# Key projections cut at column 256 instead of 272, and the gated activations' room moved by 192 bytes, in a hybrid attention block

## The chip, the cores and the metric

The kernel runs on one core of one Trainium2 chip. The metric is the device time of one execution in microseconds (us); lower is better. The time of a kernel is the median of its runs; the kernel before has three of them. A run of the profiler adds a trace: for every instruction of every engine its start, its duration and what it waited for. The engines are TensorE (PE, the matmuls; its weight loads are listed apart as PEld), VectorE (DVE), ScalarE (ACT), GpSimd (POOL) and the queue that issues the DMAs (SP).

## The reference

One decoder layer over 528 positions: 16 meta tokens ahead of 512 real ones, a model width of 1024. Cut to what matters here:

```
u = rmsnorm(h, pre_norm_g)
(cq, ckv, k_pe, z_mla, fq, fk, fv, f_logit, z_fox, gate_a, gate_b) = split(u @ w_in)
MLA: q from rmsnorm(cq) @ w_uq, k and v from rmsnorm(ckv) @ w_ukv, 16 heads, causal softmax
FoX: q, k, v = fq, fk, fv, 16 heads of 64, causal softmax with a forget gate in the logits
y_mla = (o_mla * silu(z_mla)) @ w_br_mla ;  y_fox = (o_fox * silu(z_fox)) @ w_br_fox
mixed = (sigmoid(gate_a) * y_mla + sigmoid(gate_b) * y_fox) @ w_out
out = h + rmsnorm(mixed, post_norm_g)          # the 16 meta rows are dropped
```

Everything is float32. The kernel reaches that precision by splitting each operand into a high part that TensorE takes as it is and a low part that is the rest, and by summing three products: high weights with high data, high weights with low data, low weights with high data. So every product of the reference is three matmuls in the trace, named by their operands (`fk<-uTh,wh`, `fk<-uTl,wh`, `fk<-uTh,wl`: out, then streamed operand, then stationary one).

## The kernel before

**Layout.** The normalised input lies transposed in two tiles, `uTh` and `uTl` (high and low part): 128 partitions, 8 blocks of the model dimension (`KD`), and in each block a row of 576 float32 columns, of which the first 48 are unused, the next 16 are the meta tokens and the last 512 the real positions. A row is 2304 bytes, nine times 256, and both tiles begin at a multiple of 256 bytes in the partition (17,152 and 35,584 in the program's allocation). So position 0 lies 192 bytes into a block of 256 bytes, and position 16, the first real one, at the beginning of a block; so does position 272, which is 1024 bytes further.

**Units.** `unit` emits one projection: for each slice of positions and each of the 8 blocks, three matmuls into one PSUM bank, and `done` when the slice is complete. Queries run over the 512 real positions at once. Keys and values run over all 528, which is more than a bank holds, so they are cut into two slices: `ALLT` gives positions 0 to 272 and 272 to 528. `hl_done` is the eviction of queries and keys: ScalarE copies the bank into the high half of the tile `hlk` (line 247), then VectorE subtracts that from the bank and writes the low half (line 249, in the trace under the helper's line 104). It runs once per slice.

**Attention.** The heads are taken in 8 pairs, and each pair has two stages: FoX (`br` 1), then MLA (`br` 0). TensorE's instructions are issued in the order in which the program names them; the other engines' order is made by a planner that heeds priorities. A stage begins with `scores`: three groups of PSUM banks, each filled for the two heads of the pair by turns. The first group holds the scores of query block 1 over key positions 0 to 272 and of block 3 over 0 to 240; the second block 0 over 0 to 144 and block 3 over 240 to 528; the third block 2 over 0 to 400:

```
((1, 0, 272, 0), (3, 0, CUT, 272))        # rooms acc
((0, 0, 144, 0), (3, CUT, L - CUT, 144))  # rooms b0, b1
((2, 0, 400, 0),)                         # rooms c0, c1
```

Each part is a query block, the first key position, a width and a place in the bank. A part is three sets of two matmuls (one per head): high queries with high keys, low queries with high keys, high queries with low keys. After the scores the stage fills TensorE with the projections of the next stages. In an MLA stage this filling is the next pair's FoX work, in this order: queries (8 steps), the first slice of the keys (8), the values (16), the second slice of the keys (8). So the second slice of the FoX keys is the last thing that TensorE does ahead of the scores that read them, in seven of the eight pairs; the first pair's keys are made in the opening part, with other work behind them. In a FoX stage the MLA keys are made earlier, with values and a gate projection behind them.

**Branch products.** After attention the two branches' outputs are multiplied by `w_br_mla` and `w_br_fox`. The gated activations of a branch are split into the tiles `gh` and `gl` (8 blocks of 512 columns each, 2048 bytes a row), from a pool `m2`, which is opened at byte 90,880, a multiple of 256. For the FoX branch `pair_py` computes two output blocks at a time from seven products of 256 columns by 512 rows of contraction: four of the seven stream `gh` and `gl` themselves (`A11`, `S1`, `A12`, `A22`), the other three stream sums that lie in `a1` and `a2`. There are four such pairs, so 4 x 4 x 12 = 192 matmuls of 256 columns stream `gh` or `gl`. The tiles `a1` and `a2` begin 192 bytes past a multiple of 256 (161,216 and 169,408 for their high parts). For the MLA branch `py` streams `gh` and `gl` in 192 matmuls of 512 columns. The split weights that stand in TensorE in all of these begin at multiples of 256 bytes.

The names and lines that the change touches: `KEYS` (new, beside `HALF`), `ALLT`, `hl_done` (lines 237 to 250), `k_fox` (line 255), `k_mla` (line 687), and the pool `m2` (line 1066).

Of the kernel before, what the change touches and what calls it, by code (L numbers as in the profile page):

```python
# [11 lines left out]
F32 = mybir.dt.float32  # L12
# [13 lines left out]
L = S + META  # L26
NH = 16
KD = D // 128
# [7 lines left out]
O_CQ, O_ZM, O_FQ, O_FK, O_FV, O_F, O_ZF, O_GA, O_GB = 0, 416, 1440, 2464, 3488, 4512, 4528, 5552, 6576  # L36
# [7 lines left out]
SF_STEP = 272  # L44
PN_STEP = 5
HALF = 272
CUT = 240
ROW = 64

# [6 lines left out]
def block_kernel(ctx: ExitStack, tc: tile.TileContext, x, meta_tokens, pre_norm_g, w_in, fox_forget_b,  # L56
# [32 lines left out]
    def dma(out, src, start=None):  # L89

        with tc.issue_after(sums_out[0]) if written[0] and sums_out else nullcontext():
            ins = (start or nc.sync.dma_start)(out=out, in_=src)
        if written[0]:
            tc.keep_in_program_order(ins)
        return ins.ins

    def mm(*a, **k):
        nc.tensor.matmul(*a, **k)  # L98
# [4 lines left out]
    def split_lo(eng, lo, src, hi):  # L103
        return eng.tensor_tensor(out=lo, in0=src, in1=f32(hi), op=ALU.subtract)  # L104
# [34 lines left out]
    def weights(srcs, wrap):  # L139

        st = {}

        def load():
            if "l" not in st:
                st["l"] = wload(srcs())

        def get():
            load()
            return wrap(wsplit(st["l"]))
        get.load = load  # L150
        return get

    def by_k(part, nk):

        h, l = (t.rearrange("p (k f) -> p k f", k=nk) for t in part)
        return (lambda k: h[:, k, :]), (lambda k: l[:, k, :])
# [20 lines left out]
    def unit(name, getw, act, nk, sls, done, banks=None):  # L177

        st = {}
        out = []  # L180

        def prep():
            if "w" not in st:
                st["w"] = getw()
            return True
        for i, sl in enumerate(sls):
            n = sl.stop - sl.start
            for k in range(nk):
                def fn(i=i, sl=sl, k=k, n=n):
                    if "b" not in st:  # L190
                        st["b"] = prep()
                        for load in getattr(out[0][1], "nxt", ()):
                            load()
                    if k == 0:
                        st["ps"] = (banks or acc)(f"{name}{i}")
                    ps = st["ps"][:, :n]
                    (wh, wl), (ah, al) = st["w"], act(k)
                    for q, (w, a) in enumerate(((wh, ah), (wh, al), (wl, ah))):
                        mm(ps, w(k), a[:, sl], start=(k == 0 and q == 0), stop=(k == nk - 1 and q == 2))
                    if k == nk - 1:  # L200
                        done(i, ps)
                out.append((3 * n / 2.4, fn))
        out[0][1].prep = prep
        if hasattr(getw, "load"):
            out[0][1].load = getw.load
        return out

    keybank = [None]
    REAL = [slice(META, L)]
    ALLT = [slice(0, HALF), slice(HALF, L)]  # L210

    def u_act(k):
        return uTh[:, k, :], uTl[:, k, :]
# [7 lines left out]
    def win_w(off, i):  # L221
        return weights(lambda: [win[:, :, off + 128 * i : off + 128 * i + 128]], lambda w: by_k(w[0], KD))
# [14 lines left out]
    def hl_done(key, n, w):  # L237

        def done(i, ps):
            if i == 0:  # L240
                hls[key] = hlp.tile([128, 2, n], F32R, tag=f"hl{key[0]}", name="hl" + "".join(map(str, key)))
            hl = hls[key]
            o = w * i
            w_ = min(w, n - o)

            with tc.high_priority(offset=30), tc.issue_after(normed[0]) if key == ("q", 0, 0) else nullcontext():
                halved[key, i] = nc.scalar.copy(hl[:, 0, o : o + w_], ps).ins
            with tc.high_priority(offset=30):
                lowered[key, i] = split_lo(nc.vector, hl[:, 1, o : o + w_], ps, hl[:, 0, o : o + w_]).ins
        return done  # L250
# [2 lines left out]
        return unit(f"fq{pr}", win_w(O_FQ, pr), u_act, KD, REAL, hl_done(("q", 1, pr), S, S))  # L253

    def k_fox(pr):
        return unit(f"fk{pr}", win_w(O_FK, pr), u_act, KD, ALLT, hl_done(("k", 1, pr), L, HALF), keybank[0])

# [1 line left out]
    with ExitStack() as ph:  # L261
# [246 lines left out]
        latent(2, sms[2])  # L508

        qk = q_fox(0) + k_fox(0)  # L510
        behind[:] = [squared[1]]
        run(qk[:7])
# [34 lines left out]
    with ExitStack() as att:  # L547
# [7 lines left out]
        def bank(tag):  # L555
            return lambda name: stp.tile([128, 512], F32, tag=tag, name=name)
# [4 lines left out]
        def two(tag):  # L561
            return lambda name: bank(tag + name[-1])(name)
# [121 lines left out]
        mw = {}  # L684

        def k_mla(pr):
            return unit(f"mk{pr}", lambda: by_k(mw[pr][2], 1), ckv_act, 1, ALLT, hl_done(("k", 0, pr), L, HALF), two("b"))

        vsc = {}

        def v_unit(br, pr):
# [39 lines left out]
            def tr():  # L731
                dma(vps[br], vh.rearrange("p t c -> p (t c)"), nc.sync.dma_start_transpose)
            return unit(f"v{br}{pr}", get, act, nk, ALLT, done, two("c")), [(0, tr)]

# [15 lines left out]
        def attention(br, pr):  # L750
# [46 lines left out]
            def scores():  # L797
# [3 lines left out]
                for g in range(2):  # L801
                    sfs[g] = aw.tile([128, 2, (2 * SF_STEP + 400, L)[g]], F32, tag=f"sf{g}", name=f"sf{nm_}{g}", bufs=1)
                for rooms, parts in (([acc, acc], ((1, 0, 272, 0), (3, 0, CUT, 272))),
                                     ([bank("b0"), bank("b1")], ((0, 0, 144, 0), (3, CUT, L - CUT, 144))),
                                     ([bank("c0"), bank("c1")], ((2, 0, 400, 0),))):
# [128 lines left out]
        def feed(br, pr):  # L934

            q = (q_mla, q_fox)[br](pr)
            k = (k_mla, k_fox)[br](pr)
            v, vts[br, pr] = v_unit(br, pr)
            return q, k, v
# [13 lines left out]
        for si, (br, pr) in enumerate(stages):  # L953
            last = si + 1 == len(stages)
            if not last:
                q, k, v = feed(*stages[si + 1])
# [105 lines left out]
    with ExitStack() as mg:  # L1062
# [2 lines left out]
        mgg = ExitStack()  # L1065
        m2 = mgg.enter_context(tc.tile_pool(name="m2", bufs=1))
        HK = KD // 2
        gh, gl = (m2.tile([128, KD, S], F32R, tag=n, name=n) for n in ("gh", "gl"))
        thx[0] = mgg.enter_context(tc.tile_pool(name="thx", bufs=2))
        sp = mgg.enter_context(tc.tile_pool(name="sp", bufs=5, space=PSUM))  # L1070
        tb = [m1.tile([128, HK, 512], F32, tag=f"tb{n}", name=f"tb{n}") for n in range(4)]
        a1 = [m1.tile([128, HK, 256], F32R, tag=n, name=n) for n in ("a1h", "a1l")]
        a2 = [m1.tile([128, HK, S], F32R, tag=n, name=n) for n in ("a2h", "a2l")]
        mx = gT[0]
        sh, sl = ([t.rearrange("p k s -> p (k s)")[:, 1024 * j : 1024 * j + 1024].rearrange("p (k s) -> p k s", k=HK)
                   for j in range(4)] for t in uT0)
# [6 lines left out]
        def py(i, br):  # L1083
# [8 lines left out]
            nc.vector.tensor_tensor(out=mx[:, i], in0=mx[:, i], in1=gT[1][:, i], op=ALU.add)  # L1092
            src, (h, l) = (mx[:, i, 0:256], [t[:, i] for t in a1]) if i < HK else (mx[:, i], [t[:, i - HK] for t in a2])
            nc.scalar.copy(h, src)
# [9 lines left out]
        def ssum(ks):  # L1104

            kt = slice(ks.start + HK, ks.stop + HK)
            m11, m21, m12, m22 = mx[:, ks, 0:256], mx[:, ks, 256:512], mx[:, kt, 0:256], mx[:, kt, 256:512]
# [286 lines left out]
```

## Time and profile before

| | |
|---|---|
| median of three runs | 587.31 us (587.02 to 587.46) |
| span of the profiled execution, first to last instruction | 584.6 us |
| median of the runs less that span | 2.7 us |
| PE busy | 575.7 us, 98% of the span |
| DVE, ACT, POOL busy | 71%, 61%, 34% |
| granted TensorE clock | 0.997 |

The profile gives the profiled execution's own time by its span; 2.7 us more lie ahead of the first and behind the last instruction in the median run. A matmul's listed duration is longer than the time that it takes of TensorE, since matmuls overlap: what a stream costs is the distance from its start to the start of the next one, and this is read from the timeline. A timeline row holds the start, the duration, the engine, the line, the operation, output and inputs, the shape and how many instructions were merged into the row; in brackets the idle time before it and what ended that. Line 98 is the helper of all matmuls, line 104 that of all low-part subtractions.

### The profile page before, as it was taken

Reading aid. Unit: us, or ns where it says so; the run is one execution under the profiler, and the core shown is the slowest. Engines: PE = TensorE matmul, PEld = TensorE weight load, DVE = VectorE, ACT = ScalarE, POOL = GpSimd, SP = SyncE. Lnnn points to the kernel's source line nnn. Section 1 sums busy time; section 2 is a strip of 40 time slices with the busy share of each in tenths; the row PEclk is TensorE's granted clock in tenths of the full one; section 3 lists DMA queues with packets and bytes.
Section 4 is the critical chain, followed back from the end, with each engine's and each line's share of the span. In section 5 each row is a group of like instructions: output and inputs, shape, how many; then the busy total and the mean of one; then the engine's idle time right before and its main releaser. Section 6 shows DMA issues by size and latency. Waiting matters only on the chain.

```text
span 584.6 us, 11115 instructions
## 1 busy us (share of the span) xinstructions
PE 575.7 (98%) x3841; PEld 496.8 (85%) x3841; DVE 416.4 (71%) x1156; ACT 357.4 (61%) x816; POOL 199.4 (34%) x270
## 2 busy tenths in 40 slices
PE   8999999999999999999999999999999999999996
PEld 6989889889889888888898898878998998888884
DVE  5854877885776775767758748896647876468966
ACT  7856774893774775767748747944343462443762
POOL 4317745464468462654554634510000000000000
PEclk9999999999999999999999999999999999999998
DMA  8535599989977999988986976977722534233503
GB/s 295 122 83 163 127 176 230 231 195 248 177 167 158 228 191 206 219 172 207 183 176 180 219 154 147 183 172 236 233 73 72 145 104 144 78 109 108 217 0 144
DMA packets 220000, 97.47 MB, mean 167 GB/s; under 512 B 131456, under 2 KB 209672, under 8 KB 219944
## 3 DMA queue, kind: packets, MB, share of 16 engines
q1 hardware_dynamic: 219944, 96.77, 70.3%
q8 instruction: 30, 0.49, 0.3%
q14 instruction: 26, 0.21, 0.1%
HBM read 62.36 MB, written 3.97 MB: 113 GB/s over the span
## 4 chain that ended last, share of the span: by engine, by line
PE 96%; ACT 1%; DMA 1%; issue 0%; SPq 0%; DVE 0%; POOL 0%; DVEq 0%; ACTq 0%; POOLq 0%
PE z L98 19%; PE pg L98 15%; PE v L98 9%; PE fk L98 8%; PE st L98 8%; PE fq L98 8%; PE x L98 8%; PE py L98 7%; PE ov L98 5%; PE psm L98 3%; PE y L98 2%; PE mq L98 2%; PE mk L98 1%; PE ppe L98 1%; DMA wsr<-in_w_in_dram 1%; ACT uTh L371 0%
## 5 line engine op out<-in xcount | busy, mean ns | idle before, releaser
L104 POOL TENSOR_TENSOR wl<-wraw,wh 128x1024 fp32r<-128x1024 f32 (+2 forms) x61 | 118.3, 1947 | 112.2 <-ACT wh L131 80.5
L131 ACT CAST wh<-wraw 128x1024 fp32r<-128x1024 f32 (+1 forms) x72 | 74.6, 1042 | 56.4 <-PE py L98 16.8
L826 ACT ACTIVATE sf<-sf,nb 128x272 f32<-128x272 f32 (+3 forms) x128 | 72.7, 569 | 11.5 <-DVE nb L791 10.6
L865 DVE SCALAR_TENSOR_TENSOR pn<-sf,ri,pn 128x512 f16<-128x512 f32 (+3 forms) x128 | 69.6, 609 | 1.6 <-ACT pn L861 1.5
L104 DVE TENSOR_TENSOR wl<-wraw,wh 128x512 fp32r<-128x512 f32 (+1 forms) x55 | 52.2, 950 | 23.9 <-ACT wh L1119 17.8
L861 ACT ACTIVATE pn<-sf,ri 128x128 f16<-128x128 f32 (+3 forms) x128 | 59.7, 548 | 0.5 <-DVE ri L831 0.5
L98 PE MATMUL z<-uTh,wh 128*128 128x512 f32 x128 | 50.9, 398 | 0.0
L98 PE MATMUL pg<-uTh,wh 128*128 128x512 f32 x128 | 50.2, 392 | 0.0
L98 PE MATMUL z<-uTl,wh 128*128 128x512 f32 x128 | 50.1, 391 | 0.0
L98 PE MATMUL z<-uTh,wl 128*128 128x512 f32 x128 | 50.0, 390 | 0.0
L98 PE MATMUL pg<-uTl,wh 128*128 128x512 f32 x128 | 49.9, 390 | 0.0
L98 PE MATMUL pg<-uTh,wl 128*128 128x512 f32 x128 | 49.8, 389 | 0.0
L706 DVE TENSOR_REDUCE vsc<-v 128x1 f32<-128x272 f32 (+1 forms) x32 | 13.2, 433 | 39.8 <-PE v L98 39.8
L98 PE MATMUL st<-hlk,hlq 64*128 64x272 f32 (+4 forms) x480 | 41.3, 299 | 0.0
L1119 ACT CAST wh<-wraw 128x512 fp32r<-128x512 f32 x28 | 17.3, 618 | 37.9 <-DVE wraw L1128 17.0
L98 PE MATMUL v<-uTh,wl 128*128 128x256 f32 (+1 forms) x128 | 36.5, 285 | 0.0
L98 PE MATMUL fk<-uTl,wh 128*128 128x256 f32 (+1 forms) x128 | 36.4, 285 | 0.0
L98 PEld LDWEIGHTS st<-hlk,hlq 64*128 64x128 f32 x480 | 33.0, 186 | 4.1 <-ACT vh L725 2.8
L98 PE MATMUL fk<-uTh,wh 128*128 128x256 f32 (+1 forms) x128 | 36.4, 285 | 0.0
L98 PE MATMUL v<-uTl,wh 128*128 128x256 f32 (+1 forms) x128 | 36.4, 285 | 0.0
L98 PE MATMUL fk<-uTh,wl 128*128 128x256 f32 (+1 forms) x128 | 36.4, 285 | 0.0
L98 PE MATMUL v<-uTh,wh 128*128 128x256 f32 (+1 forms) x128 | 36.4, 284 | 0.0
(295 smaller groups left out, 1612.3 us busy)
## 6 DMA issues: line engine op xcount, KB each, us to landing
wraw<-in_w_in_dram SPq DMA_DIRECT2D x56, 512.0 KB, 4.8
cbp<-c_dram SPq DMA_DIRECT2D x16, 264.0 KB, 4.1
wraw<-in_w_br_fox_dram SPq DMA_DIRECT2D x8, 512.0 KB, 4.5
tb<-in_w_out_dram SPq DMA_DIRECT2D x8, 512.0 KB, 5.4
wraw<-in_w_br_mla_dram SPq DMA_DIRECT2D x8, 512.0 KB, 4.3
wraw<-in_w_out_dram SPq DMA_DIRECT2D x6, 512.0 KB, 3.6
xr<-in_x_dram SPq DMA_DIRECT2D x4, 512.0 KB
out_dram<-yo SPq DMA_DIRECT2D x8, 256.0 KB, 2.0
```

The lines of the kernel that those rows point to most:

```text
L98: nc.tensor.matmul(*a, **k)
L104: return eng.tensor_tensor(out=lo, in0=src, in1=f32(hi), op=ALU.subtract)
L131: nc.scalar.copy(wh[:, :n], raw[:, :n])
L706: nc.vector.tensor_reduce(out=sc[:, i : i + 1], in_=ps, op=ALU.max, axis=AX.X, apply_absolute_value=True)
L826: exps[b // 3] = nc.scalar.activation(sf, sf, AF.Exp, bias=sums["nb"][:, h, b : b + 1], scale=-1.0, accum_out=sums["su"][:, h, b : b + 1]).ins
L861: normed[:] = [nc.scalar.activation(hi, sf, AF.Copy, scale=rib).ins]
L865: nc.vector.scalar_tensor_tensor(out=lo, in0=sf, scalar=rib, in1=hi, op0=ALU.mult, op1=ALU.subtract)
L1119: nc.scalar.copy(to[0], src)
```

## The change

The keys of both branches are cut at position 256 instead of 272: the first slice is 256 columns wide and the second 272. `hl_done` is told the width of the first slice and gives the second one all that is left. The values keep the old cut. In the pool `m2` a tile of 48 float32 columns (192 bytes) is allocated ahead of `gh` and `gl` and never used, so these two, and the tiles of the next pool behind them, move up by 192 bytes.

```
+KEYS = 256
...
+    KEYT = [slice(0, KEYS), slice(KEYS, L)]
...
-            w_ = min(w, n - o)
+            w_ = n - o if i else w
...
-        return unit(f"fk{pr}", win_w(O_FK, pr), u_act, KD, ALLT, hl_done(("k", 1, pr), L, HALF), keybank[0])
+        return unit(f"fk{pr}", win_w(O_FK, pr), u_act, KD, KEYT, hl_done(("k", 1, pr), L, KEYS), keybank[0])
...
-            return unit(f"mk{pr}", lambda: by_k(mw[pr][2], 1), ckv_act, 1, ALLT, hl_done(("k", 0, pr), L, HALF), two("b"))
+            return unit(f"mk{pr}", lambda: by_k(mw[pr][2], 1), ckv_act, 1, KEYT, hl_done(("k", 0, pr), L, KEYS), two("b"))
...
         HK = KD // 2
+        m2.tile([128, 48], F32, tag="m2pad", name="m2pad")
         gh, gl = (m2.tile([128, KD, S], F32R, tag=n, name=n) for n in ("gh", "gl"))
```

The parts of `scores` are not changed.

## The prediction

> **What bounds the kernel now.** I read the page first, for the engines and the chain of work that ended last.
>
> ```profile
> span 584.6 us, 11115 instructions
> ...
> PE 575.7 (98%) x3841; PEld 496.8 (85%) x3841; DVE 416.4 (71%) x1156; ACT 357.4 (61%) x816; POOL 199.4 (34%) x270
> ...
> PE 96%; ACT 1%; DMA 1%; issue 0%; SPq 0%; DVE 0%; POOL 0%; DVEq 0%; ACTq 0%; POOLq 0%
> PE z L98 19%; PE pg L98 15%; PE v L98 9%; PE fk L98 8%; PE st L98 8%; PE fq L98 8%; PE x L98 8%; PE py L98 7%; PE ov L98 5%; PE psm L98 3%; PE y L98 2%; PE mq L98 2%; PE mk L98 1%; PE ppe L98 1%; DMA wsr<-in_w_in_dram 1%; ACT uTh L371 0%
> ```
>
> TensorE is 96% of the chain, in all stages. Next the list of waits, for TensorE's matmuls over the whole span, and one row of the list for its weight loads.
>
> ```profile
> PE spun L98 <- DVE KPL L234: 1.4, 1, 1.4
> PE psm L98 <- POOL wsh L302: 1.0, 1, 1.0
> PE pc L101 <- ACT st L321: 0.4, 1, 0.4
> PE pt L101 <- DVE hn L347: 0.3, 1, 0.3
> ...
> PEld st L98 <- ACT vh L725: 2.8, 8, 0.4
> ```
>
> These four are all the waits of matmuls there are, 3.1 us, and they belong to the opening; asked from 41 us on, the same list is empty. From then on TensorE streams without a wait, so the time is the sum of the distances between its matmuls: a matmul that takes fewer ns shortens the end by as much, and a new wait lengthens it by as much. The change removes and adds no instruction and no DMA, and moves no step past a queue. It changes where streams begin, how wide the key slices are, and which slice holds positions 256 to 271.
>
> **Part 1: streams that begin at byte 192.** The groups by line and shape show matmuls of one width with two durations.
>
> ```profile
> L98 PE MATMUL z<-gh,wh 128*128 128x256 f32 x16 | 4.5, 283 | 0.0
> ...
> L98 PE MATMUL z<-a2h,wh 128*128 128x256 f32 x16 | 4.4, 276 | 0.0
> ```
>
> Both write the same kind of bank and stand on weights that begin at a multiple of 256; `gh` begins at a multiple of 256 bytes, `a2h` 192 bytes past one. The distances are in TensorE's timeline, of which I give the first and the last row of a run for each case.
>
> ```profile
> 89.22 0.29 PE L98 MATMUL fk<-uTh,wl 128*128 128x272 f32 x1
> ...
> 90.94 0.29 PE L98 MATMUL fk<-uTl,wh 128*128 128x272 f32 x1
> ...
> 99.32 0.28 PE L98 MATMUL fk<-uTl,wh 128*128 128x256 f32 x1
> ...
> 100.52 0.28 PE L98 MATMUL fk<-uTh,wl 128*128 128x256 f32 x1
> ...
> 429.54 0.28 PE L98 MATMUL x<-gh,wh 128*128 128x256 f32 x1
> ...
> 431.94 0.28 PE L98 MATMUL z<-gh,wl 128*128 128x256 f32 x1
> 435.21 0.28 PE L98 MATMUL x<-a2h,wh 128*128 128x256 f32 x1
> ...
> 437.48 0.28 PE L98 MATMUL z<-a2h,wl 128*128 128x256 f32 x1
> ...
> 502.96 0.39 PE L98 MATMUL py<-gh,wh 128*128 128x512 f32 x1
> ...
> 503.87 0.39 PE L98 MATMUL py<-gl,wh 128*128 128x512 f32 x1
> ```
>
> A FoX key stream of 272 columns at byte 192 costs 1.72 us / 14 = 123 ns; one of 256 columns at byte 0, 1.20 / 10 = 120 ns; a stream of `gh` or `gl`, 256 columns at byte 0, 2.40 / 20 = 120 ns; `a2`, 256 columns at byte 192, 2.27 / 20 = 113.5 ns; `py`, 512 columns at byte 0, 0.91 / 4 = 227 ns. So 256 columns cost 6.5 ns less where they begin at byte 192.
>
> Two groups of 256 columns get that start. FoX keys: 8 pairs x 24 = 192 matmuls; the slice of 272 keeps its start of 192 bytes (256 x 4 = 1024 bytes further is the same place in a block) and its 123 ns. Products of `gh` and `gl` in pairs: 4 x 4 x 12 = 192. Together 384 x 6.5 ns = 2.5 us; I take 2.4, since the first streams after a change of width are not all at 120 ns now. Bounds: 0, if place in the block is not what sets the two spacings, and 2.6, at 113.3 ns, below which no run of 256-column streams on this weight layout stays.
>
> By the Trainium skill ("TensorE: Matmul & The Clock Gate", Back-to-back issue gap) the gap is N / 2.4 + 2.5 ns, wherever a stream begins: an estimate of 109 ns for 256 columns and nothing gained by this part. The rows speak against it, with 120 and 113.5 ns for one width; the rule's case is the second rival below.
>
> The 192 streams of `py` move to byte 192 too, and no row has 512 columns there on weights at byte 0. The nearest:
>
> ```profile
> L98 PE MATMUL py<-gh,wh 128*128 128x512 f32 x64 | 24.9, 389 | 0.0
> L98 PE MATMUL x<-wh,a1l 128*128 128x512 f32 x8 | 3.2, 394 | 0.0
> L98 PE MATMUL mq<-cTl,wh 128*128 128x512 f32 x16 | 6.3, 395 | 0.0
> L98 PE MATMUL mk<-cTl,wh 128*128 128x272 f32 x8 | 2.4, 294 | 0.0
> L98 PE MATMUL mk<-cTh,wh 128*128 128x256 f32 x8 | 2.3, 283 | 0.0
> ```
>
> Where stream and weights lie differently in their blocks the matmul is listed up to 6 ns longer: 192 x 6 = 1.2 us lost at most. A gain I exclude: 227 ns for 512 columns is 0.443 ns a column, what 256 columns reach at their best (113.5 / 256). I take 0, since the nearest row in width and place, 113.5 x 2 = 227, is what `py` costs now. The MLA keys (48 matmuls) exchange widths over other starts; rows between 283 and 294 bound them at 48 x 11 ns = 0.5 us either way, and I take 0.
>
> **Part 2: positions 256 to 271 go to the second slice.** The first part of `scores` reads key positions 0 to 272. Now these are exactly the first slice, whose eviction lies behind the values' matmuls. After the change 16 of them are in the second slice, the last thing that TensorE makes before a FoX stage's scores, in seven of the eight pairs. The cover goes. The timeline of all engines at such a place (pair 1), then the evictions of a slice of 272 (pair 7), then a fresh start of TensorE behind another engine:
>
> ```profile
> 100.84 0.37 ACT L247 CAST hlk<-fk 128x256 fp32r<-128x256 f32 x1 [0.57 <-PE fk L98]
> 101.24 0.42 DVE L104 TENSOR_TENSOR hlk<-fk,hlk 128x256 fp32r<-128x256 f32 x1 [0.29 <-ACT hlk L247]
> ...
> 101.09 0.39 PE L98 MATMUL st<-hlk,hlq 64*128 64x272 f32 x4
> ...
> 101.83 0.47 PE L98 MATMUL st<-hlk,hlq 64*128 64x288 f32 x4
> ...
> 341.17 0.39 ACT L247 CAST hlk<-fk 128x272 fp32r<-128x272 f32 x1 [1.61 <-PE fk L98]
> 341.59 0.44 DVE L104 TENSOR_TENSOR hlk<-fk,hlk 128x272 fp32r<-128x272 f32 x1 [1.30 <-ACT hlk L247]
> ...
> 7.91 0.90 POOL L302 CAST wsh<-wsr 128x864 fp32r<-128x864 f32 x1 [6.13 <-DMA wsr<-in_w_in_dram]
> 8.87 0.47 PE L98 MATMUL psm<-wsh,uTh 128*128 128x432 f32 x1 [0.96 <-POOL wsh L302]
> ```
>
> Now: the last key matmul starts at 100.52, the first score set that reads low keys (the third) at 101.09, 0.57 us later. The second slice's low half is ready at 101.24 + 0.42 = 101.66, and its first reader, the 288-wide part, starts at 101.83. The cover is 0.17 us wide.
>
> After: counted from the start of the last key matmul, the stream is 16 columns longer (0.01), so ScalarE's copy starts at 0.33 instead of 0.32; it takes 0.39 (0.72), VectorE follows 0.03 later (0.75) and takes 0.44 (1.19), and TensorE starts 0.06 after that, as behind POOL (8.87 less 8.81): 1.25. The first two sets want the copy alone, from 0.78 on, and fit in between. The third set, due at 0.57, runs at 1.25: **0.68 us** late, and 7 x 0.68 = **4.8 us**. Behind the waiting matmul stands everything that TensorE has, since its order is fixed; the bank's readers on VectorE, the exponentials on ScalarE and the transposes on SP wait with it and keep their distances. Bounds for one stall: 0.60 (no start-up, evictions at their fastest) and 0.80 (TensorE loses another 0.1 in restarting), so 4.2 to 5.6 us. The first pair pays nothing: its keys are covered by the opening's projections. Nor do the MLA stages, which have values and a gate behind their keys. The evictions' 16 columns more or less, 0.02 us each, lie under matmuls elsewhere.
>
> **The sum.** -2.4 + 4.8 = +2.4 us. Against the profile: 584.6 + 2.4 = 587.0; the median run lies 2.7 above the span (587.31 less 584.6), so **589.7 us**, 0.4% above the runs shown. Its own range: from 4.2 - 2.6 = +1.6 to 5.6 - 2.4 + 0.9 = +4.1, the 0.9 being about half of what `py` and the MLA keys could lose together (1.7); that is 588.9 to 591.4.
>
> **The rivals.**
>
> *The starts bring nothing.* Then `a2` and `gh` differ by something else, and the stalls stand alone: 587.3 + 4.8 = **592.1**. For it: `gh` and `a2` also lie in different parts of the memory. Against: `uTh` keys, in yet another part, have the 120 ns of `gh` where they share its place in the block.
>
> *The stall is given back, not slower.* The mechanism is the weight load's wait for `vh` ahead of the MLA scores, 0.35 us in each of eight stages (2.8 / 8). If TensorE really stood there, it would, arriving 0.68 late, find `vh` ready and get 0.35 back: 7 x 0.35 = 2.4 us, which leaves 587.3 + 2.4 - 2.4 = **587.3**, no change. It decides from 2.4 / 7 = 0.34 us per stage on. Against: the wait is the weight load's, and no matmul waits there.
>
> *The copy queues behind a weight cast.* At pair 7 ScalarE's next work after the key copy is a weight cast of 1.05 us:
>
> ```profile
> 350.15 1.05 ACT L131 CAST wh<-wraw 128x1024 fp32r<-128x1024 f32 x1
> ```
>
> If the planner puts it first, the stall becomes 1.7 us; in four of seven pairs that is 589.7 + 4.2 = **594**. Against: the copy's priority is raised, and it comes first in each pair now.
>
> **How the numbers follow.** Forecast 0.74; starts bring nothing 0.10; given back 0.08; cast first 0.08. The range reaches down into the third case's partial forms and up to take in the second: **588.4 to 592.4**, which leaves out most of the last two cases and the forecast's edges. About 0.2% (1.2 us) is what a measurement of this kernel can tell from no change. Slower by more: nearly all of the forecast, the starts-bring-nothing case and the cast-first case, 0.90; within: the given-back case, 0.07; faster, were the wait shorter than any row allows: 0.03.
>
> **What would show it.** In the changed profile: seven new waits of `st` on `hlk` (line 104, perhaps line 247 ahead of it) in TensorE's list, 0.5 to 0.8 us each, where now there is none; FoX keys of 256 columns at 113 to 114 ns, beside 272 at 123; `x`, `y`, `z` from `gh` at 113 to 114 instead of 120; `py` still at 227. The forecast is wrong if TensorE's list stays empty after 41 us, if the third score set starts within 0.7 us of the last key matmul, or if `gh` streams keep 120 ns.

## The result, and the profile after

| | before | after |
|---|---|---|
| median of the runs | 587.28 us (587.02 to 587.46) | 593.79 us (593.07 to 594.47) |
| ratio, 95% interval | | 1.0103 (1.0085 to 1.0121) |
| span of the profiled execution | 584.6 us | 592.4 us |
| DVE, ACT, POOL busy | 416.4, 357.4, 199.4 us | 416.7, 357.4, 200.5 us |

The change makes the kernel 6.5 us slower, the way that was forecast but by far more than the 2.4 us of the forecast and beyond the range. The other engines' work is the same to within 1.1 us, so I looked at TensorE again. The list of its waits after (the lines of the changed kernel are numbered one to three higher):

```profile
PE st L99 <- ACT hlk L249: 3.3, 7, 0.5
PE psm L99 <- POOL wsh L304: 1.8, 1, 1.8
PE spun L99 <- DVE KPL L236: 1.5, 1, 1.5
PE pc L102 <- ACT st L323: 0.4, 1, 0.4
```

The first row is new: seven waits of score matmuls for the key tile. The second is the opening, where TensorE waited 1.8 us instead of 1.0 for a cast of the first weights. The first FoX key matmul starts at 42.73 us here and at 41.65 in the kernel before; in the other nine traces of this document it starts between 41.37 and 42.19, with either key cut. So I put these 1.1 us down to this one execution, though the other executions of the changed kernel have no trace. They explain most of why the spans differ by 7.8 us and the medians by 6.5.

The list for the weight loads has these rows of scores:

```profile
PEld st L99 <- ACT hlk L249: 4.8, 7, 0.7
PEld st L99 <- ACT vh L727: 2.8, 8, 0.4
PEld st L99 <- DVE hlk L105: 1.3, 7, 0.2
```

The third row is a second wait in each of the seven stages, for the low half that VectorE writes; the list of the matmuls does not have it.

The timeline at the same place as in the prediction, pair 1, from the last key matmul to the fourth score set:

```profile
101.40 0.29 PE L99 MATMUL fk<-uTh,wl 128*128 128x272 f32 x1
...
101.72 0.39 ACT L249 CAST hlk<-fk 128x272 fp32r<-128x272 f32 x1 [0.67 <-PE fk L99]
102.14 0.44 DVE L105 TENSOR_TENSOR hlk<-fk,hlk 128x272 fp32r<-128x272 f32 x1 [0.40 <-ACT hlk L249]
...
102.16 0.39 PE L99 MATMUL st<-hlk,hlq 64*128 64x272 f32 x2 [0.47 <-ACT hlk L249]
...
102.64 0.50 PE L99 MATMUL st<-hlk,hlq 64*128 64x272 f32 x4
...
102.87 0.49 PE L99 MATMUL st<-hlk,hlq 64*128 64x240 f32 x6
```

The scores begin 0.05 us after ScalarE's copy has ended (101.72 + 0.39 = 102.11), and the third set, which reads the low half, 0.06 after VectorE's subtraction (102.14 + 0.44 = 102.58). Counted from the last key matmul the third set starts at 1.24; the prediction had 1.25. The fourth set follows the third by 0.23, where before it followed by 0.12. The rows of before for it:

```profile
101.09 0.39 PE L98 MATMUL st<-hlk,hlq 64*128 64x272 f32 x4
...
101.21 0.50 PE L98 MATMUL st<-hlk,hlq 64*128 64x240 f32 x6
```

So the fourth set is late by 1.47 - 0.69 = 0.78 us, and 7 x 0.78 = 5.5. The list of the matmuls' waits shows only 3.3 of it: it counts time in which no matmul is in flight, and leaves out the second wait and the slower start of the set behind it.

The streams. First and last rows of runs: FoX keys of 256 columns, at byte 192 now; `gh` and `gl` entered from a gate projection; `a2`, which the change did not move; `py`.

```profile
90.11 0.28 PE L99 MATMUL fk<-uTh,wl 128*128 128x256 f32 x1
...
92.47 0.28 PE L99 MATMUL fk<-uTl,wh 128*128 128x256 f32 x1
...
435.09 0.39 PE L99 MATMUL pg<-uTh,wl 128*128 128x512 f32 x1
435.32 0.28 PE L99 MATMUL x<-gh,wh 128*128 128x256 f32 x1
...
437.91 0.28 PE L99 MATMUL z<-gl,wh 128*128 128x256 f32 x1
...
441.09 0.28 PE L99 MATMUL x<-a2l,wh 128*128 128x256 f32 x1
...
443.32 0.28 PE L99 MATMUL z<-a2h,wl 128*128 128x256 f32 x1
...
501.14 0.39 PE L99 MATMUL py<-gh,wh 128*128 128x512 f32 x1
...
502.07 0.39 PE L99 MATMUL py<-gl,wh 128*128 128x512 f32 x1
```

FoX keys: 2.36 / 20 = 118 ns, not 113.5. `gh` and `gl`: 2.59 / 22 = 118 ns. `a2`: 2.23 / 19 = 117 ns, where before it had 113.5 at the same address, on weights at the same address. `py`: 0.93 / 4 = 233 ns instead of 227.

To see where the time went I summed, in both traces, the distance from each matmul's start to the next one's, by what it streams:

| | before, us | after, us | difference |
|---|---|---|---|
| scores, and the last key matmul ahead of them | 47.08 | 52.51 | +5.43 |
| `py`, 192 streams of 512 | 43.52 | 44.80 | +1.28 |
| `a1` and `a2` products, 144 streams of 256 | 16.47 | 16.96 | +0.49 |
| `gh` and `gl` products, 192 streams of 256 | 22.86 | 22.61 | -0.25 |
| FoX keys, the other 377 matmuls | 45.87 | 45.41 | -0.46 |
| sum | | | +6.49 |

The difference of the medians is 6.51. Another 0.2 us lies in 48 streams of `wh` and `wl`, 512 columns on weights in `a1` and `a2`. Neither stream nor weights moved, but these matmuls come straight behind `py`: they take 229 ns on the mean before and 233 after. With the 1.1 of this execution's opening that makes the 7.8 between the spans.

### The profile page after: what moved, and what is told of

Its sections match the earlier page's. It is cut to its first block, busy times and chain, and to the rows that moved or that the text cites. A ratio compares the mean times of both kernels' runs of the same rounds, so it can differ in the third digit from the quotient of the medians.

```text
span 592.4 us, 11115 instructions
## 1 busy us (share of the span) xinstructions
PE 579.7 (98%) x3841; PEld 497.1 (84%) x3841; DVE 416.7 (70%) x1156; ACT 357.4 (60%) x816; POOL 200.5 (34%) x270
## 4 chain that ended last, share of the span: by engine, by line
PE 95%; ACT 2%; DMA 1%; issue 0%; SPq 0%; DVE 0%; POOL 0%; DVEq 0%; ACTq 0%; POOLq 0%
PE z L99 19%; PE pg L99 15%; PE v L99 9%; PE st L99 8%; PE fk L99 8%; PE fq L99 8%; PE py L99 8%; PE x L99 8%; PE ov L99 5%; PE psm L99 3%; PE y L99 2%; PE mq L99 2%; DMA wsr<-in_w_in_dram 1%; PE mk L99 1%; PE ppe L99 1%; ACT hlk L249 0%
## 5 line engine op out<-in xcount | busy, mean ns | idle before, releaser
L99 PE MATMUL st<-hlk,hlq 64*128 64x272 f32 (+4 forms) x480 | 42.8, 302 | 3.3 <-ACT hlk L249 3.3
L99 PE MATMUL fk<-uTh,wh 128*128 128x272 f32 (+1 forms) x128 | 36.4, 284 | 0.0
L99 PE MATMUL fk<-uTh,wl 128*128 128x272 f32 (+1 forms) x128 | 36.3, 284 | 0.0
L99 PE MATMUL fk<-uTl,wh 128*128 128x272 f32 (+1 forms) x128 | 36.3, 283 | 0.0
```

## The experiments

Times beside the experiments are medians of runs on one chip each, together with runs of the kernel before on the same chip, whose median was 587.13 us in the first four experiments, 587.17 in the next four and 587.20 in the last. Two theories had to be told apart for each part of the sum.

**The key cut alone.**

```
-        m2.tile([128, 48], F32, tag="m2pad", name="m2pad")
```

> Only the keys' cut moves to 256; gh and gl stay at byte 0. Theory A (after the result): the stalls cost 7 x 0.785 = 5.5 us, the key streams of 256 columns at 117.7 instead of 120 ns give back 0.5, the opening is not touched: +5.0 us against the kernel before, 592.3, ratio 1.0085; py at 227 ns and the a1 and a2 streams at 114 to 115 ns on the mean, as before. Theory B (the changed kernel's later opening, 1.1 us in its profiled execution, comes from the key cut): +6.1, 593.4.

Measured: 592.24 us, ratio 1.0084 (1.0071 to 1.0098). Theory A had 592.3. TensorE's whole list of waits:

```profile
PE st L99 <- ACT hlk L249: 3.3, 7, 0.5
PE spun L99 <- DVE KPL L236: 1.4, 1, 1.4
PE pc L102 <- ACT st L323: 0.4, 1, 0.4
```

The seven stalls are there and the opening's wait for POOL is not: the first FoX key matmul starts at 41.67 us, against 41.65 before. The later opening is not of the key cut's making.

**The move of `gh` and `gl` alone**, with the keys cut at 272.

```
         HK = KD // 2
+        m2.tile([128, 48], F32, tag="m2pad", name="m2pad")
```

> Only gh and gl move by 192 bytes; the keys are cut at 272. Theory A: py's 192 streams at 233.3 instead of 226.7 ns cost 1.3 us, a1 and a2 streams at 117.7 instead of 114.6 cost 0.5, gh and gl of 256 columns at 117.7 instead of 119 give 0.25: +1.5 us, 588.8, ratio 1.0026, and no wait of TensorE behind 41 us. Theory of the prediction (256 columns at byte 192 at 113.5, py unchanged): -1.1 us, 586.2.

Measured: 588.69 us, ratio 1.0027 (1.0017 to 1.0038); theory A had 588.8, and the prediction's own price 586.2. No stall behind the opening. The group of `py` in this run:

```profile
L98 PE MATMUL py<-gh,wh 128*128 128x512 f32 x64 | 25.2, 394 | 0.0
```

against 24.9 and 389 before; its distances are 233.3 ns on the mean, those of `a1` and `a2` 117.7. The two parts add up: 5.1 and 1.6 us against 6.5 of both together.

**The key cut, with the 16 positions read later.** In the FoX stages of pairs 1 to 7 block 1's scores are split at column 256, and the last 16 columns come behind block 0's scores.

```
+                        if br and pr and b == 1:
+                            emit(b, 0, KEYS, 0, ps)
+                            later.append((b, KEYS, w - KEYS, KEYS, ps))
+                            continue
...
+                        if later and b == 0:
+                            emit(*later.pop())
+                            evict(kept.pop())
```

> Key cut at 256 without the move of gh and gl, but in the FoX stages of pairs 1 to 7 block 1's scores over positions 256 to 271 are computed behind block 0's, as three more sets of 16 columns, and the first bank is read after that. Theory A (the stall is the wait for those 16 positions): no wait of TensorE on hlk, the extra sets cost 7 x 0.2 = 1.4 us, the key streams give 0.5: +0.9 us, 588.2. Rival (the second slice's eviction is in the way wherever the 16 positions are read, by its longer hold of ScalarE and VectorE): the waits stay, +5 us or more.

Measured: 588.46 us, ratio 1.0023 (1.0014 to 1.0032). TensorE's whole list of waits, and the group of the added matmuls:

```profile
PE spun L99 <- DVE KPL L236: 1.4, 1, 1.4
PE pc L102 <- ACT st L323: 0.4, 1, 0.4
PE psm L99 <- POOL wsh L304: 0.4, 1, 0.4
...
L99 PE MATMUL st<-hlk,hlq 64*128 64x16 f32 x42 | 3.1, 240 | 0.0
```

No score waits for a key any more, with the same cut and the same eviction. The scores' sum of distances is 2.3 us above that of before, 0.33 a stage for the 42 added matmuls instead of the 0.2 that I had put. So the stall is the wait for positions 256 to 271; the second slice's eviction by itself, read later, holds nothing up.

**Why 117.7 and not 113.3.** In the kernel before, the `a1` and `a2` streams always came behind `gh` streams at byte 0. Its timeline where `a1` follows `gh`:

```profile
431.94 0.28 PE L98 MATMUL z<-gh,wl 128*128 128x256 f32 x1
432.06 0.29 PE L98 MATMUL x<-a1h,wh 128*128 128x256 f32 x1
432.18 0.28 PE L98 MATMUL x<-a1l,wh 128*128 128x256 f32 x1
432.30 0.28 PE L98 MATMUL x<-a1h,wl 128*128 128x256 f32 x1
432.41 0.28 PE L98 MATMUL x<-a1h,wh 128*128 128x256 f32 x1
...
433.32 0.28 PE L98 MATMUL x<-a1h,wl 128*128 128x256 f32 x1
```

Two distances of 0.12 to the next, then 0.11, and from 432.41 on 0.91 / 8 = 114 ns. After the change they come behind streams at 118 and keep to 118. Theory H: the spacing that a run of streams settles at hangs on what it was entered from. Theory P: the place alone sets it.

A first try added a tile of 192 bytes to the pool of `a1` and `a2` as well, but ahead of them:

```
+        m1.tile([128, 48], F32, tag="m1pad", name="m1pad")
         tb = [m1.tile([128, HK, 512], F32, tag=f"tb{n}", name=f"tb{n}") for n in range(4)]
```

> Keys as before; gh and gl at byte 192, and a1 and a2 moved from byte 192 to byte 0. Theory H (a stream's spacing hangs on how the run of streams was entered: behind 256-column streams at byte 0 those at byte 192 settle at 113.3 ns, behind 512-column streams at 117.7): the products A11 and S1, entered from a gate projection, at 117.7, the products of a1 and a2 at 120, A12 and A22 behind them at 113.3 on the mean 115. Theory P (the place alone sets it): all gh and gl products of 256 columns at 117.7. In both py at 233: +1.8 to +2.3 us, about 589.3.

Measured: 588.42 us, ratio 1.0019 (1.0010 to 1.0028). The pool grows downwards from its fixed upper end, so a tile ahead of the others moves none of them: `a1` and `a2` stayed at byte 192, against what the expectation says. All distances of this stage are those of the move alone, 117.7 and 233.3. It decides nothing between H and P, and shows that a repetition comes out within 0.3 us.

With the tile behind them instead, and `gh` and `gl` still at byte 192, `a1` and `a2` do move to byte 0:

```
         a2 = [m1.tile([128, HK, S], F32R, tag=n, name=n) for n in ("a2h", "a2l")]
+        m1.tile([128, 48], F32, tag="m1pad", name="m1pad")
```

> Keys as before; gh and gl at byte 192, a1 and a2 now at byte 0 (the tile of 192 bytes lies behind them). Theory H (the spacing hangs on how the run of streams was entered: behind 256-column streams at byte 0, which run at 120 ns, those at byte 192 settle at 113.3; behind 512-column streams at 117.7): A11 and S1 at 117.7, the a1 and a2 products at 119 to 120, A12 and A22 behind them near 113.3 after three slower ones; py at 233; +1.4 us, 588.5. Theory P (place alone): A12 and A22 at 117.7 too, +1.8, 588.9.

Measured: 588.68 us, ratio 1.0027 (1.0018 to 1.0036): in time between H and P. The timeline decides. Here `gh` at byte 192 follows `a1` at byte 0 (product A12):

```profile
434.10 0.28 PE L98 MATMUL x<-a1h,wl 128*128 128x256 f32 x1
434.22 0.29 PE L98 MATMUL y<-gh,wh 128*128 128x256 f32 x1
434.35 0.28 PE L98 MATMUL y<-gl,wh 128*128 128x256 f32 x1
434.47 0.28 PE L98 MATMUL y<-gh,wl 128*128 128x256 f32 x1
434.58 0.28 PE L98 MATMUL y<-gh,wh 128*128 128x256 f32 x1
...
435.49 0.28 PE L98 MATMUL y<-gh,wl 128*128 128x256 f32 x1
```

From 434.58 on 0.91 / 8 = 114 ns, while A11 and S1 in the same tile, at the same byte, entered from a gate projection, run at 117.7 in this trace. The distances of A12 are 121, 122, 116, 114, 113, 113, the row of `a1` in the kernel before. Theory H holds, theory P falls.

**A layout made by theory H.** For the products in pairs A11 alone lies at byte 0, the rest at byte 192; for `py` every row lies at byte 0.

```
-        gh, gl = (m2.tile([128, KD, S], F32R, tag=n, name=n) for n in ("gh", "gl"))
+        gr = [m2.tile([128, KD * S + 64], F32R, tag=n, name=n) for n in ("gh", "gl")]
+        gh, gl = (t[:, 0 : KD * S].rearrange("p (k s) -> p k s", k=KD) for t in gr)
...
-        A11, A12, A22, S1 = ([t[:, kb[q], ts] for t in (gh, gl)] for q, ts in ((0, lo_), (1, lo_), (1, up), (0, up)))
+        A11, A12, A22, S1 = ([t[:, o : o + 1024].rearrange("p (k s) -> p k s", k=HK) for t in gr] for o in (0, 1072, 2096, 3120))
```

> Keys as before; for the products in pairs the room of gh and gl is laid out so that A11 begins at byte 0 and S1, A12 and A22 at byte 192, for py all rows lie at byte 0 as before. Theory H: A11 at 120, and from S1 on all of a pair's products at 113.3, py at 226.7: -0.9 us against the kernel before, 586.2, ratio 0.9985. Theory P: S1, A12, A22, a1 and a2 at 117.7: +0.25, 587.4.

Measured: 586.45 us, ratio 0.9991 (0.9980 to 1.0003), not clear of the kernel before by itself. In the trace the pairs' sum of distances is 38.45 us instead of 39.33, which is the 0.9 expected, with S1 and all behind it at 113.3 to 115.1 and `py` at 226.7.

**Other places.** The tile ahead of `gh` and `gl` made 64 and 128 bytes long, with the keys cut at 272 (the edit at 64 bytes, against the kernel before; at 128 it is 32 columns):

```
         HK = KD // 2
+        m2.tile([128, 16], F32, tag="m2pad", name="m2pad")
```

> Keys as before; gh and gl moved by 64 bytes instead of 192. If only equal places of stream and weights keep 512 columns at 226.7 ns, py lies at 230 to 234 (+0.6 to +1.4 us) as at byte 192. If byte 192 alone is bad for 512 columns, py stays at 227 and the time within 0.5 us of the kernel before. Theory H makes no forecast for 256 columns at byte 64 but that a1 and a2, entered from another spacing, need not run at 113.3.

> As the run at 64 bytes, with gh and gl moved by 128 bytes. If only equal places of stream and weights keep 512 columns at 226.7 ns, py lies at 230 to 234 (+0.6 to +1.4 us); if byte 192 alone is bad, at 227. The products of 256 columns are bounded by 113.3 and 120 ns either way.

Measured: 587.69 us, ratio 1.0005 (0.9996 to 1.0014) at 64 bytes; 588.30 us, ratio 1.0020 (1.0011 to 1.0029) at 128. `py` in the two, first 64, then 128:

```profile
L98 PE MATMUL py<-gh,wh 128*128 128x512 f32 x64 | 25.2, 394 | 0.0
L98 PE MATMUL py<-gl,wh 128*128 128x512 f32 x64 | 24.9, 388 | 0.0
```

```profile
L98 PE MATMUL py<-gh,wh 128*128 128x512 f32 x64 | 25.3, 395 | 0.0
L98 PE MATMUL py<-gl,wh 128*128 128x512 f32 x64 | 25.3, 395 | 0.0
```

The mean distance is 226.7 ns at byte 0, 229.1 at 64, 233.3 at 128 and at 192. So of these four places `py`, on weights at byte 0, is fastest where its streams begin at the same place in their blocks; at 64 bytes it comes out just under the 230 that I had as the lower end. The 256-column products summed to 39.6 us at byte 64, 39.4 at 128 and 39.6 at 192. The unmoved `a1` and `a2` streams behind them settled near 117.7 ns in the run at 64 bytes and at 113.4 in the run at 128, so byte 0 is not the only entry to the faster spacing.

**A shorter entry.** Of A11 only the first of four blocks, three matmuls, at byte 0 (shown against the layout made by theory H; a line in `prod` that picks the block is left out):

```
-        A11, A12, A22, S1 = ([t[:, o : o + 1024].rearrange("p (k s) -> p k s", k=HK) for t in gr] for o in (0, 1072, 2096, 3120))
+        A12, A22, S1 = ([t[:, o : o + 1024].rearrange("p (k s) -> p k s", k=HK) for t in gr] for o in (1072, 2096, 3120))
+        head, rest = ([t[:, o : o + 256 * n].rearrange("p (k s) -> p k s", k=n) for t in gr] for o, n in ((0, 1), (304, 3)))
+        A11 = [lambda k, h=h, r=r: h[:, 0] if k == 0 else r[:, k - 1] for h, r in zip(head, rest)]
...
-            split_to(A11, g11)
+            split_to(head, g11[:, 0:1])
+            split_to(rest, g11[:, 1:])
```

> As the run with A11 at byte 0, but of A11 only the first of its four blocks (three matmuls of twelve) lies at byte 0, the other three at byte 192 like S1, A12 and A22. Theory H with a short entry (three matmuls at byte 0 behind a gate projection are enough, since their distances there are 114, 119 and 120 already): A11 runs 114, 119, 120, 121, 121, 116 and from the seventh on at 113.3, and so does all that follows: 0.24 us less in the pairs than with all of A11 at byte 0, 1.1 less than before: 586.1, ratio 0.998. Theory H with a long entry (a run must have settled at 120 ns first): the streams at byte 192 settle at 117.7, and the pairs cost as much as in the kernel with the move alone, 39.6 us in the sum of distances: 587.4.

Measured: 586.09 us, ratio 0.9984 (0.9975 to 0.9993), 0.2% faster than the kernel before, and so faster than both kernels. Its timeline from the gate projection on:

```profile
429.16 0.39 PE L98 MATMUL pg<-uTh,wl 128*128 128x512 f32 x1
429.38 0.28 PE L98 MATMUL x<-gh,wh 128*128 128x256 f32 x1
429.50 0.28 PE L98 MATMUL x<-gl,wh 128*128 128x256 f32 x1
429.62 0.28 PE L98 MATMUL x<-gh,wl 128*128 128x256 f32 x1
429.74 0.29 PE L98 MATMUL x<-gh,wh 128*128 128x256 f32 x1
429.86 0.28 PE L98 MATMUL x<-gl,wh 128*128 128x256 f32 x1
429.98 0.28 PE L98 MATMUL x<-gh,wl 128*128 128x256 f32 x1
430.10 0.28 PE L98 MATMUL x<-gh,wh 128*128 128x256 f32 x1
...
431.91 0.28 PE L98 MATMUL z<-gl,wh 128*128 128x256 f32 x1
```

Six distances of 0.12, and from 430.10 on 1.81 / 16 = 113 ns. Three streams at byte 0 are enough to enter the faster spacing; with the whole room at byte 192, as after the change, it is never entered. The pairs' sum is 38.20 us, 1.1 below the kernel before, which is also the difference of the medians.

## Why the prediction was right or wrong

**What bounds the kernel: right.** TensorE's distances make the time: their differences sum to 6.5 us in the table and 6.7 with the streams behind `py`; the medians differ by 6.5. The forecast missed 4.1 us of this: 2.2 in the price of the starts, 1.3 in `py`, 0.6 in the stall.

**Part 2, the stall: right in mechanism, place and count, its size short by 0.6 us.** Seven stalls, on positions 256 to 271, in the stages named; the third set starts within 0.01 us of the predicted time. The failed term is the stop there: the prediction took the third set's lateness, 0.68, for that of all behind it, and held a loss of 0.1 in restarting for a bound. It is the rule: the fourth set comes 0.23 instead of 0.12 us behind the third, in all seven stages. The scores' row of the table has 5.4 us instead of 4.8.

**Part 1, "256 columns cost 6.5 ns less where they begin at byte 192": wrong.** The step read a price off `a2`, and took its place for the cause without its history. The moved streams settled at 117.7 ns; the keys gained 0.46 us and `gh` and `gl` 0.25, and the 144 unmoved streams of `a1` and `a2` lost 0.49, which no step had asked about: taking `gh` off byte 0 took away what they were entered from. In all 0.2 us gained instead of 2.4. The rival in which the starts bring nothing came nearer. The Trainium skill ("TensorE: Matmul & The Clock Gate", Back-to-back issue gap) gives N / 2.4 + 2.5 ns for the isolated gap and says that in a stream of weight loads and matmuls both set the spacing; the 109 ns worked out from the formula for 256 columns no run here shows.

**`py` at no cost: wrong.** The value was taken by doubling the 256-column price, 113.5 x 2 = 227, as if the two widths had one cause; the row called nearest has half the width. The rows of 512 columns, 394 and 395 ns on other places, were the better ones: 233.3 ns, +1.28 us, just above the 1.2 that they gave as a bound. The 0.2 us of the streams behind `py` no step had asked about either.

**The MLA keys and the evictions at no cost: right.** The MLA keys' sum changed by less than 0.1 us, and the first pair had no stall.

**The range** failed with these: its upper end, 592.4, held the stall at its bound or no gain from the starts, but not the stall's restart, no gain and `py`'s loss together, and these three came together. The rival without any gain, 592.1, was nearest in mechanism. The cast-first rival's 594 is nearest as a number, by luck: it fell, since ScalarE's copy starts 0.32 us behind the start of the last key matmul in each of the seven stages. The given-back rival fell too: the weight loads' wait for `vh` is 2.8 us in eight stages as before, and nothing came back.

## What to carry to other kernels

Where one engine streams without a wait, a slice boundary is a schedule: before a cut is moved, look which later instruction reads across the new one, and how far behind the producing slice it stands. A stall costs the wait and the restart behind it, 0.1 us here. The list of the matmuls' waits shows neither the second wait nor the restart, and the second wait stands only in the list of the weight loads, so measure a stall by start times on both sides. A spacing read off some streams is a price only for streams with the same neighbours; one run that makes the move alone is worth more than rows of other operands.

## What the runs showed of the hardware that was not expected

Float32 streams of 256 columns at byte 192 of a block, on weights at byte 0, have two steady spacings: 113.3 ns when entered from a few streams of 256 columns at byte 0 (in one run at byte 128), and 117.7 ns when entered from streams of 512 columns. In the runs above 117.7 was kept for all 84 products between two gate projections, and 113.3 for 78. At byte 0 the spacing is 120.0 ns from the third stream behind a gate projection on. The 512-column streams of `py` take 226.7, 229.1, 233.3 and 233.3 ns on the mean at bytes 0, 64, 128 and 192. History matters at this width too: the same 48 streams on `a1` and `a2` take 229 ns behind `py` at 226.7 and 233 behind `py` at 233.3. Whether `py`'s own 233.3 hangs on what it was entered from was not tried; it came behind a gate projection in every run. What in the memory or in the loading of weights makes this is not settled: the runs show that start place, width and history matter, not by what.
